# Storing q, k, y and the gate z as the vector engine leaves them, placing blocks at the load, and softmax sums sent to the gate through DRAM

## The chip, the cores and the metric

The kernel runs on one core of a Trainium2 chip. The metric is the time of one execution in device microseconds, the median of several runs. The engines are named as the profile names them: PE (matmul, with PEld for its weight loads), DVE (vector), ACT (scalar), POOL (GpSimd) and SP, which here does nothing but issue DMAs. All scratch tensors between the phases lie in the chip's DRAM (HBM).

## The reference

Two layers (DEPTH = 2) run over 2048 latent tokens and 256 context tokens of width 1024. A layer normalises and modulates the tokens, multiplies them by one input matrix (3344 columns), splits the columns among three groups of heads, and multiplies the concatenated outputs by one output matrix (condensed):

```python
(au, av, az, bq, bk, bv, bz, cq, ck, cv, co, cz, cg) = _split_proj(xn @ w_in)
y_b = softmax(q_lat @ k_all.T * scale) @ v_all * silu(bz)      # 8 heads of 64, 2 kv heads
y_c = sigmoid(co) * rms_norm(h_forward + h_backward) * silu(cz)  # mLSTM, 4 heads of 64
y_a = gelu(au) * (w_s @ layer_norm(gelu(av)) + b_s) * silu(az)   # gated MLP, 4 groups of 64
x = x + gt * (concatenate([y_a, y_b, y_c]) @ w_out)
```

Latent tokens attend to context and latent tokens (2304 keys), context tokens to the context alone, and the last layer has no context output.

## The kernel before

Tokens are cut into 18 tiles of 128 (2 of context, 16 latent), and tiles into blocks: the two context tiles, then four blocks of four latent tiles. A layer has three phases, and the next one's first work overlaps the last one's end.

**proj_phase** multiplies. It goes three times over six tiles each (a macro), and in each over seven groups of columns; a group's result for a tile is finished by a function of its own (post_c1 for the mLSTM's q and k, post_a2 for u and the attention's k, post_b1 for q, post_b2 for the gate z, ...), which ends with a store to DRAM through `ld`, so on SP's queue. Later phases want q, k and y transposed, with the features on partitions. DVE's transpose works on 32 by 32 blocks and leaves the blocks where they were, so `put_blocks` stores a tile with four DMAs, one for each group of 32 partitions, and each DMA puts its blocks of 128-byte pieces where they belong. During the third macro the mLSTM runs as well: `ml_state` walks over the tiles in both directions, and `ml_out` makes a tile's output. An ml_out loads sc, sct, sst, soz and two broadcast rows of snm (tile xt), POOL masks those rows, ACT exponentiates them, PE and DVE do the rest, and put_y stores the tile's y with eight of the DMAs of put_blocks (two chunks of 128 columns). At most three ml_out are alive at a time.

**attn_phase** works in units of one head and one block (32 a layer, and 8 for the context in the first layer). `unit_s` makes the scores of a unit (PE, 40 matmuls), DVE scales them and finds the maximum, ACT exponentiates and gives each row's sum (`den`). `unit_tr` transposes 128 keys of the unit on PE (18 steps of four transposes), and the copy is split in a rounded part and a rest: on odd steps by POOL (pT, lines 1119 and 1120), on even ones by DVE. `unit_mm` multiplies with v, five steps behind (LAG = 5). `unit_end` gates: for a pair of heads z is loaded as rows of tokens (tile sz), POOL multiplies each of the up to four tiles by 0.5/den (line 1148, the sum is a scalar of each partition there), PE transposes the gated z (line 1157), and DVE multiplies the output O with it.

**out_phase** loads a tile's y (tile yr, one DMA), splits it in two parts, multiplies with w_out, adds the residual.

PE multiplies fp32r with each operand split in two parts. The order of all instructions on an engine is fixed when the kernel is built, by a scheduler that simulates a timeline, so an engine that waits holds up everything behind it in its own order. SP too works its DMAs off in order, and a DMA whose data or buffer is not ready holds up those behind it.

## Time and profile before

| what | value |
|---|---|
| median of 3 runs | 3683.24 us (3678.11 to 3684.99) |
| the profiled execution: time, span | 3684.58 us, 3682.9 us |
| PE, DVE, ACT, POOL busy | 3582.6, 2556.9, 1942.0, 1892.3 us |
| granted clock of PE, mean | 0.988 |
| DMA packets | 531690, of them 297274 under 512 B |

The span runs from the first to the last instruction, and 1.7 us of the execution's time lie outside it. The first attention phase fills about 900 to 1700 us, the second about 2690 to 3470 us. The stretches in which the third macro and the mLSTM share the engines are about 640 to 920 us and 2480 to 2710 us. In the kernel before, line numbers of the profile are those of the listing above.

### The profile page before, as it was taken

How to read it: one execution, taken by the hardware profiler on the slowest of the kernel's cores; microseconds unless marked ns; L12 is line 12 of the kernel's file. 1: busy time of each engine (PE TensorE's matmuls, PEld its weight loads, DVE VectorE, ACT ScalarE, POOL GpSimd, SP SyncE). 2: the span in 40 equal slices, each digit the busy share in tenths (PEclk: the TensorE clock that was granted, in tenths of full speed). 3: DMA queues.
4: the chain of work that ended last, by engine and by line, in shares of the span. 5: the costliest groups of instructions: out<-in, count | busy, mean ns of one | idle time of the engine just before them, and what ended most of it. 6: DMA issues, size and time to landing. Idle time of an engine off the chain costs nothing.

```text
span 3682.9 us, 58371 instructions
## 1 busy us (share of the span) xinstructions
PE 3582.6 (97%) x19405; PEld 2937.3 (80%) x19405; DVE 2556.9 (69%) x6341; ACT 1942.0 (53%) x3409; POOL 1892.3 (51%) x2448
## 2 busy tenths in 40 slices
PE   8999999998999999999999999999999999999999
PEld 4877778776888888887788788877778888888787
DVE  4676664778888888887324636466888888888754
ACT  4223243334878788786114432432377877777621
POOL 2241342454777777776322524244557777777610
PEclk9999999999999999999999999999999999999999
DMA  7456455576001011002545553557720101100143
GB/s 216 137 138 175 138 129 136 159 194 156 25 28 37 17 35 43 24 12 95 175 121 151 132 148 83 141 145 180 174 57 18 31 27 35 35 24 10 58 148 113
DMA packets 531690, 359.21 MB, mean 98 GB/s; under 512 B 297274, under 2 KB 432178, under 8 KB 531388
## 3 DMA queue, kind: packets, MB, share of 16 engines
q1 hardware_dynamic: 518172, 336.05, 33.8%
q10 hardware_dynamic: 10368, 9.52, 0.8%
q0 software_dynamic: 2848, 9.91, 0.7%
q8 instruction: 154, 2.52, 0.3%
q14 instruction: 148, 1.21, 0.1%
HBM read 269.56 MB, written 85.76 MB: 96 GB/s over the span
## 4 chain that ended last, share of the span: by engine, by line
PE 69%; DMA 6%; DVE 4%; POOL 3%; issue 2%; SPq 2%; ACT 2%; DVEq 0%; POOLq 0%; ACTq 0%
PE acc L209 20%; PE m L1131 14%; PE acc L1096 14%; PE tr L1113 9%; PE x L209 6%; PE x L1113 4%; SPq L53 2%; DMA raw<-in_w_in_dram 1%; DMA xt<-snm 1%; DMA mkv<-sc 1%; DMA tab<-in_rope_dram 1%; DVE w L200 1%; DVE e L1098 1%; PE tr L476 0%; POOL pT L1120 0%
## 5 line engine op out<-in xcount | busy, mean ns | idle before, releaser
L209 PE MATMUL acc<-w,xn 128*128 128x512 f32 (+2 forms) x4728 | 1096.5, 385 | 5.3 <-POOL w L203 1.7
L209 PEld LDWEIGHTS acc<-w,xn 128*128 128x128 f32 x4728 | 844.2, 191 | 182.8 <-issue 5.4
L1098 DVE TENSOR_SCALAR_CACHE_REDUCE e<-acc,rqall 128x512 f32<-128x512 f32 (+1 forms) x1296 | 858.1, 690 | 144.4 <-PE acc L1096 76.6
L1131 PE MATMUL m<-pT,vst 128*128 128x512 f32 (+1 forms) x2336 | 775.3, 415 | 4.8 <-POOL pT L1120 4.0
L1096 PE MATMUL acc<-kst,qs 128*128 128x512 f32 (+1 forms) x2592 | 744.5, 385 | 11.6 <-DVE e L1098 10.0
L1120 POOL TENSOR_TENSOR pT<-pf,pT 128x512 fp32r<-128x512 f32 (+1 forms) x564 | 730.5, 1302 | 29.7
L1104 ACT ACTIVATE e<-e,nmx 128x2304 f32<-128x2304 f32 (+1 forms) x272 | 578.5, 2127 | 61.4 <-DVE nmx L1103 60.7
L1119 POOL TENSOR_SCALAR pT<-pf 128x512 fp32r<-128x512 f32 (+1 forms) x564 | 356.8, 636 | 338.5 <-ACT pf L1118 332.9
L1096 PEld LDWEIGHTS acc<-kst,qs 128*128 128x128 f32 x2592 | 447.4, 189 | 92.1 <-DVE e L1098 21.7
L1131 PEld LDWEIGHTS m<-pT,vst 128*128 128x128 f32 x2336 | 411.7, 189 | 65.6 <-POOL pT L1120 8.6
L1113 PE MATMUL tr<-ident,e 128*128 128x128 f32 x3084 | 456.9, 273 | 3.0 <-DVE pT L1123 2.1
L1113 PEld LDWEIGHTS tr<-ident,e 128*128 128x128 f32 x3084 | 375.1, 141 | 79.1 <-DVE pT L1123 4.0
L200 DVE TENSOR_TENSOR w<-raw,w 128x512 fp32r<-128x512 f32 (+1 forms) x276 | 205.5, 755 | 184.0 <-ACT w L199 182.3
L199 ACT CAST w<-raw 128x512 fp32r<-128x512 f32 (+1 forms) x276 | 161.6, 595 | 299.0 <-DMA raw<-in_w_in_dram 265.1
L1123 DVE TENSOR_TENSOR pT<-tr,pT 128x512 fp32r<-128x512 f32 x405 | 274.2, 683 | 59.5 <-ACT pT L1122 58.4
L209 PE MATMUL acc<-w,xs 128*128 128x512 f32 x1224 | 294.2, 398 | 1.7 <-DVE xs L249 1.3
L1122 ACT CAST pT<-tr 128x512 fp32r<-128x512 f32 x405 | 234.4, 587 | 95.2 <-PE tr L1113 79.8
L209 PEld LDWEIGHTS acc<-w,xs 128*128 128x128 f32 x1224 | 230.9, 189 | 58.3 <-DVE xs L249 1.7
L209 PE MATMUL x<-w,xn 128*128 128x512 f32 (+1 forms) x1128 | 263.3, 379 | 10.4 <-DVE w L200 6.0
L1118 ACT COPY pf<-tr 128x512 f32<-128x512 f32 (+1 forms) x372 | 214.5, 584 | 87.1 <-PE tr L1113 77.8
L202 POOL TENSOR_SCALAR w<-raw 128x512 fp32r<-128x512 f32 (+1 forms) x92 | 65.5, 712 | 361.7 <-PE acc L209 158.7
L209 PEld LDWEIGHTS x<-w,xn 128*128 128x128 f32 x1128 | 200.1, 190 | 54.8 <-DVE w L200 8.9
(282 smaller groups left out, 4402.9 us busy)
## 6 DMA issues: line engine op xcount, KB each, us to landing
raw<-in_w_in_dram SPq DMA_DIRECT2D x240, 256.0 KB, 3.1
raw<-in_w_in_dram SPq DMA_DIRECT2D x144, 128.0 KB, 2.4
mkv<-sc SPq DMA_DIRECT2D x68, 258.0 KB, 4.0
xt<-snm SPq DMA_DIRECT2D x68, 256.0 KB, 4.5
yr<-sy SPq DMA_DIRECT2D x34, 512.0 KB, 6.5
mst<-in_w_ada_dram SPq DMA_DIRECT2D x64, 256.0 KB, 3.7
qd<-sq SPq DMA_DIRECT2D x128, 128.0 KB, 2.8
xres<-xnew POOLq DMA_DIRECT2D x18, 512.0 KB, 5.2
```

The costliest lines, as they stand in the source:

```text
L200: V.tensor_tensor(wt[:, 1, :n], raw[:, :n], wt[:, 0, :n].bitcast(F32), op=ALU.subtract)
L209: T.matmul(acc[:, :n], xs[:, a, k, :], ws[k][:, b, c0:c0 + n], start=(k == 0 and j == 0), stop=(k == KC - 1 and j == 2))
L1096: T.matmul(acc[:, 0:w], u['qs'][:, r, j * P:(j + 1) * P], kf[:, c0:c0 + w], start=(r == 0), stop=(r == 1))
L1098: V.tensor_scalar(e[:, c0:c0 + w], acc[:, 0:w], rqall[:, u['tiles'][j], u['h']:u['h'] + 1], None, op0=ALU.mult, op1=ALU.max, accum_out=mx[ ...
L1104: A.activation(e[:, 0:nk], e[:, 0:nk], AF.Exp, bias=nmx, scale=1.0, accum_out=u['den'][:, j:j + 1])
L1113: T.transpose(tr[:, j * P:(j + 1) * P], u['e'][j][:, s * P:(s + 1) * P], ident)
L1118: A.copy(pf[:, 0:w], tr[:, 0:w])
L1119: G.tensor_scalar(pt_[:, 0, 0:w], pf[:, 0:w], 1.0, 0.0, op0=ALU.mult, op1=ALU.add)
L1120: G.tensor_tensor(pt_[:, 1, 0:w], pf[:, 0:w], pt_[:, 0, 0:w].bitcast(F32), op=ALU.subtract)
L1122: A.copy(pt_[:, 0, 0:w], tr[:, 0:w])
L1123: V.tensor_tensor(pt_[:, 1, 0:w], tr[:, 0:w], pt_[:, 0, 0:w].bitcast(F32), op=ALU.subtract)
L1131: T.matmul(u['o'][:, 0:w], vst[u['g']][:, s, :], pt_[:, r, 0:w], start=(s == 0 and r == 0), stop=(s == u['nk'] - 1 and r == 1))
```

## The change

Tiles that DVE has transposed by blocks are stored with one DMA, as they lie, and whoever loads them puts the blocks in place. For q and k, `load_twice` takes four DMAs of 128-byte pieces in place of two DMAs of whole rows. y of the groups A and C goes into one tensor for each tile (s_y) and is loaded with four DMAs (get_blocks) and one for the attention's y; the output matrix's rows are taken in the order YC to fit. The stores of the mLSTM's q and k keep four DMAs, with another layout in DRAM, and their load reads whole rows. The gate z is transposed by blocks on DVE after post_b2 and stored like q. In unit_end it is loaded already with features on partitions, by four DMAs, so the sums must lie along the free dimension: POOL doubles den, DVE takes the reciprocal, one DMA writes it to DRAM in pieces of 4 bytes (s_den), another reads it back as a row on 64 partitions (tile rd, two buffers), and POOL multiplies z by it. The transposes on PE are gone.

```diff
-    def put_blocks(rows, t):
-        for a in range(4):
-            o = slice(a * 32, a * 32 + 32)
-            ld(rows.rearrange("(b r) t -> r b t", r=32)[:, :, o], t[o].rearrange("r (b c) -> r b c", c=32))
+    def get_blocks(dst, src):
+        v = src.rearrange("(a r) (b n) -> r b a n", a=4, b=4)
+        for b in range(4):
+            ld(dst[b * 32:b * 32 + 32].rearrange("r (a n) -> r a n", a=4), v[:, b])
...
             def load_y(i):
-                yrs[i] = pt([P, KC, P], "yr", 2)
-                ld(yrs[i], part(g_y, i).rearrange("(k p) t -> p k t", p=P))
+                yrs[i] = pt([P, KC * P], "yr", 2)
+                get_blocks(yrs[i][:, 0:512], s_y[i])
+                ld(yrs[i][:, 512:1024].rearrange("p (k t) -> p k t", k=4), part4(g_y, i))
...
             def split_y(i):
-                A.copy(xs[:, 0], yrs[i])
-                V.tensor_tensor(xs[:, 1], yrs[i], xs[:, 0].bitcast(F32), op=ALU.subtract)
+                for sl, src in ((slice(0, 4), yrs[i][:, 0:512].rearrange("p (a k c) -> p k a c", a=4, k=4)),
+                                (slice(4, 8), yrs[i][:, 512:1024].rearrange("p (k a c) -> p k a c", a=4, k=4))):
+                    hi, lo = (xs[:, q, sl].rearrange("p k (a c) -> p k a c", a=4) for q in range(2))
+                    A.copy(hi, src)
+                    V.tensor_tensor(lo, src, hi.bitcast(F32), op=ALU.subtract)
...
             def put_y(i, t, chunk, kt=None):
-                V.transpose(yt[:, 0:256], t)
-                put_blocks(part(g_y, i)[chunk * P:(chunk + 2) * P], yt[:, 0:256])
+                yv = yt[:, 0:256].rearrange("p (b x c) -> p x b c", b=4, x=2)
+                V.transpose(yv, t[:, 0:256].rearrange("p (x b c) -> p x b c", b=4, x=2))
+                o = 0 if chunk == 0 else 64
+                ld(s_y[i].rearrange("p (b n) -> p b n", b=4)[:, :, o:o + 64],
+                   yt[:, 0:256].rearrange("p (b n) -> p b n", b=4))
                 if kt is not None:
                     V.transpose(yt[:, 256:384], kt)
-                    put_blocks(part(g_k, i), yt[:, 256:384])
+                    ld(row(g_k, i), yt[:, 256:384])
...
             def post_b1(i, acc, full):
                 V.transpose(sq, q.rearrange("p h d -> p (h d)"))
-                put_blocks(part(g_q, i), sq)
+                ld(row(g_q, i), sq)
...
             def post_b2(i, acc, full):
                 V.scalar_tensor_tensor(z, th, 1.0, acc, op0=ALU.add, op1=ALU.mult)
-                ld(part(g_z, i), z)
+                V.transpose(th, z)
+                ld(row(g_z, i), th)
...
             def load_twice(dst, src, n):
-                for q in range(2):
-                    ld(dst[q * HD:(q + 1) * HD, 0:n], src.rearrange("p a b -> p (a b)"))
+                v = src.rearrange("j (a r) (b c) -> r b (j a) c", a=4, c=32)
+                for q in range(4):
+                    ld(dst[q * 32:q * 32 + 32, 0:n].rearrange("r (a c) -> r a c", c=32), v[:, q % 2])
...
             def unit_end(u):
                 if q == 0:
-                    sz = pt([P, 4, P], "sz", 3)
-                    ld(sz[:, 0:n], g_z[b][:, :, u['h'] * HD:(u['h'] + 2) * HD])
-                    pairs[b] = sz, pt([P, 512], "O", 3)
-                V.reciprocal(u['den'][:, 0:n], u['den'][:, 0:n])
-                for j in range(n):
-                    G.tensor_scalar(sz[:, j, q * HD:(q + 1) * HD], sz[:, j, q * HD:(q + 1) * HD],
-                                    u['den'][:, j:j + 1], 0.5, op0=ALU.mult, op1=ALU.mult)
+                    z = pt([P, 512], "z", 3)
+                    zv = g_z[b].rearrange("j (a r) (b c) -> r b (j a) c", a=4, c=32)
+                    for k in range(4):
+                        ld(z[k * 32:k * 32 + 32, 0:w].rearrange("r (a c) -> r a c", c=32), zv[:, 2 * u['h'] + k])
+                    pairs[b] = z, pt([P, 512], "O", 3), pt([P, 512], "rd", 2)
+                G.tensor_scalar(u['den'][:, 0:n], u['den'][:, 0:n], 2.0, None, op0=ALU.mult)
+                V.reciprocal(u['den'][:, 0:n], u['den'][:, 0:n])
+                ld(s_den[b][u['h']].rearrange("o (j p) -> (o p) j", p=P), u['den'][:, 0:n])
+                ld(rd[r, 0:w], s_den[b][u['h']].to_broadcast([64, w]))
                 A.copy(O[r, 0:w], u['o'][rx, 0:w])
                 V.tensor_tensor(O[r, 0:w], u['o'][r, 0:w], O[r, 0:w], op=ALU.add)
+                G.tensor_tensor(z[r, 0:w], z[r, 0:w], rd[r, 0:w], op=ALU.mult)
                 if q == 1:
-                    tr = ptr()
-                    for j in range(n):
-                        T.transpose(tr[:, j * P:(j + 1) * P], sz[:, j, :], ident)
-                    V.tensor_tensor(O[:, 0:w], tr[:, 0:w], O[:, 0:w], op=ALU.mult)
+                    V.tensor_tensor(O[:, 0:w], z[:, 0:w], O[:, 0:w], op=ALU.mult)
```

SP's order, at the place where the third macro of the second layer and the mLSTM run together. The kernel before has this (sy and sq are stores of y and q from the tiles k, x4 stands for four DMAs; tab, raw, msc and mst are loads):

```order
L53 DMA m_5763_28359<-soz_173 128x256
L53 DMA sy_119<-k_5764_28387 32x8x32 x4
L53 DMA tab_28421<-in_rope_dram 128x128
L53 DMA sy_120<-k_5774_28441 32x8x32 x4
L53 DMA raw_28494<-in_w_in_dram 128x512
L53 DMA raw_28499<-in_w_in_dram 128x512
L53 DMA sq_111<-k_5744_28274 32x16x32 x4
L53 DMA msc_28501<-sct_143 128x4x128
```

After the change the same tiles (k_5764, k_5744) are stored so:

```order
L53 DMA xt_28121<-snm_271 128x512
L53 DMA sya_164<-k_5764_28316 512x1x64
L53 DMA sq_106<-k_5744_28206 128x512
L53 DMA mst_28184<-sst_4_238 128x2x65
L53 DMA mst_28184<-sst_4_256 128x2x65
L53 DMA m_5733_28124<-soz_230 128x256
L53 DMA raw_28414<-in_w_in_dram 128x512
```

Each x4 has become one DMA, and the loads behind it have moved up.

POOL's order in the first attention phase, where a unit ends. Before (pT are the split copies of the transposed scores, sz the gate):

```order
L1120 TENSOR_TENSOR pT_11932<-pf_11933,pT_11932 128x512
L1148 TENSOR_SCALAR sz_12515<-sz_12515,den_11645 128x64 x4
L1119 TENSOR_SCALAR pT_11971<-pf_11972 128x512
L1119 TENSOR_SCALAR pT_12001<-pf_12002 128x512
L1120 TENSOR_TENSOR pT_11971<-pf_11972,pT_11971 128x512
```

After, for the next unit of the same pair of heads:

```order
L1181 TENSOR_SCALAR den_11870<-den_11870 128x4
L1150 TENSOR_SCALAR pT_12156<-pf_12157 128x512
L1151 TENSOR_TENSOR pT_12156<-pf_12157,pT_12156 128x512
L1150 TENSOR_SCALAR pT_12197<-pf_12198 128x512
L1151 TENSOR_TENSOR pT_12197<-pf_12198,pT_12197 128x512
L1187 TENSOR_TENSOR z_12421<-z_12421,rd_12427 64x512
L1150 TENSOR_SCALAR pT_12227<-pf_12228 128x512
```

The four products have become one short instruction ahead of two pT pairs and one product behind them, which waits for rd; in 52 of the 72 units two pairs lie between, in 14 one or none, in 6 three or more. SP's order there has the way through DRAM among the loads of q and k for later units (qd) and of the next gate (z):

```order
L53 DMA rd_12427<-sden_0_136 64x512
L53 DMA qd_13350<-sk_152 32x8x32 x3
L53 DMA sy_177<-O_11787 128x512
L53 DMA qd_13350<-sk_152 32x8x32
L53 DMA sden_1_137<-den_11870 128x4x1
L53 DMA z_13754<-sz_111 32x16x32 x2
L53 DMA rd_12427<-sden_1_137 64x512
L53 DMA z_13754<-sz_111 32x16x32 x2
```

sden writes the sums to DRAM and rd reads them back, with two DMAs of the next z between; before, none of the two was there.

## Rows read from the trace of the kernel before

**Rows 1.** the page: busy us by engine over the span; the granted clock in 40 slices

```profile
PE 3582.6 (97%) x19405; PEld 2937.3 (80%) x19405; DVE 2556.9 (69%) x6341; ACT 1942.0 (53%) x3409; POOL 1892.3 (51%) x2448
...
PEclk9999999999999999999999999999999999999999
```

**Rows 2.** busy time by stretch: length, PE, PEld, DVE, ACT, POOL, clock, DMA

```profile
640.00:920.00 280.00, 256.48 (x1508) 199.43 (x1507) 214.68 (x598) 104.19 (x276) 136.45 (x199) 0.96 0.67 173
920.00:1680.00 760.00, 757.55 (x4551) 640.38 (x4550) 647.42 (x1776) 604.68 (x896) 559.62 (x683) 1.00 0.09 27
...
2480.00:2710.00 230.00, 213.90 (x1203) 167.15 (x1200) 183.60 (x502) 85.53 (x209) 109.04 (x155) 0.94 0.65 163
2710.00:3450.00 740.00, 739.36 (x4449) 628.93 (x4447) 615.32 (x1686) 585.33 (x837) 543.27 (x654) 1.00 0.08 24
```

**Rows 3.** chain of waits in 640 to 920 us, shares by line

```profile
by line: PE acc L209 15.3%; SPq L53 11.4%; DMA xt<-snm 9.5%; issue 8.0%; DMA mkv<-sc 6.7%; DMA sy<-k 3.0%; DMA tab<-in_rope_dram 2.3%; DVE xt L813 1.8%; DMA sst<-st 1.7%; DVE e L1098 1.7%; DMA gqb<-in_g_q_dram 1.6%; DMA vr<-sv 1.5%; ACT xt 
```

**Rows 4.** waits in 640 to 920 us: total us, times, longest

```profile
POOL xt L797 <- DMA xt<-snm: 33.4, 15, 5.5
...
POOL m L764 <- DMA mkv<-sc: 21.3, 10, 4.9
...
DVE k L615 <- POOL kss L131: 18.1, 6, 4.9
```

**Rows 5.** timeline of SP, 2600 to 2640 us: start, us, DMAs issued

```profile
2613.22 1.91 SPq L53 DMA_DIRECT2D sy<-k  x4
2615.40 0.35 SPq L53 DMA_DIRECT2D tab<-in_rope_dram  x1
2616.03 1.99 SPq L53 DMA_DIRECT2D sy<-k  x4
```

**Rows 6.** DMA issues in 640 to 920 us: count, KB, median us to landing

```profile
xt<-snm SPq DMA_DIRECT2D x32, 256.0 KB, 4.6
...
sy<-k SPq DMA_DIRECT2D x96, 32.0 KB, 2.1
...
sq<-k SPq DMA_DIRECT2D x24, 64.0 KB, 3.4
...
sk<-k SPq DMA_DIRECT2D x24, 16.0 KB, 2.8
```

**Rows 7.** timeline of PE in the first attention phase: start, us, instructions

```profile
970.61 0.60 PE L1157 MATMUL tr<-ident,sz 128*128 128x128 f32 x4
970.97 0.37 PE L1131 MATMUL m<-pT,vst 128*128 128x256 f32 x1
```

**Rows 8.** instructions on the tile sz: ns min/median/max

```profile
L1157 PE MATMUL tr<-ident,sz x96: 270/272/273, 970.6 to 3502.4; 128*128 128x128 f32 x96
...
L1157 PE MATMUL x<-ident,sz x40: 270/272/273, 1080.9 to 3355.6; 128*128 128x128 f32 x40
```

**Rows 9.** the page of DMA issues over the whole span

```profile
qd<-sq SPq DMA_DIRECT2D x128, 128.0 KB, 2.8
...
sq<-k SPq DMA_DIRECT2D x136, 64.0 KB, 2.2
...
sst<-st SPq DMA_DIRECT2D x68, 65.0 KB, 4.1
```

**Rows 10.** groups by line in 920 to 1680 us: busy us, mean ns, idle before

```profile
L1120 POOL TENSOR_TENSOR pT<-pf,pT 128x512 fp32r<-128x512 f32 x266 | 346.0, 1307 | 14.0
...
L1119 POOL TENSOR_SCALAR pT<-pf 128x512 fp32r<-128x512 f32 x267 | 169.9, 640 | 164.6 <-ACT pf L1118 159.8 <-DMA qd<-sq 2.6 <-PE m L1131 1.1
...
L1148 POOL TENSOR_SCALAR sz<-sz,den 128x64 f32<-128x64 f32 x134 | 41.8, 333 | 21.6 <-DVE den L1146 15.8 <-PE acc L1096 4.2 <-DVE nmx L1103 1.1
```

**Rows 11.** groups by line, whole span

```profile
L642 DVE STREAM_TRANSPOSE k<-k 128x512 f32<-128x512 f32 x34 | 24.0, 704 | 12.9 <-POOL k L600 12.7
...
L1146 DVE RECIPROCAL den<-den 128x4 f32<-128x4 f32 x64 | 11.1, 173 | 7.5 <-ACT e L1104 6.6 <-POOL pT L1120 0.6
```

**Rows 12.** instructions on the tile kst: ns min/median/max

```profile
L1067 POOL TENSOR_TENSOR kst<-qd,kst x6: 1275/1294/1567, 855.5 to 2667.9; 64x512 fp32r<-64x512 f32 x6
```

More of the change, by code (lines that the diff above doesn't have):

```diff
@@ L58, in ld, with late @@
         return r
+    def late(n=60):
+        return tc.high_priority(offset=-n)
     def nm(s):
@@ L137, in hybrid_kernel, with row, part4 @@
     where = {t: (bi, j) for bi, b in enumerate(blocks) for j, t in enumerate(b)}
-    g_z = [dram([P, len(b), 512], f"sz{i}") for i, b in enumerate(blocks)]
     g_v = [dram([P, len(b), 128], f"sv{i}") for i, b in enumerate(blocks)]
-    g_q = [dram([512, len(b), P], f"sq{i}") for i, b in enumerate(blocks)]
-    g_k = [dram([P, len(b), P], f"sk{i}") for i, b in enumerate(blocks)]
-    g_y = [dram([D, len(b), P], f"sy{i}") for i, b in enumerate(blocks)]
+    g_q = [dram([len(b), P, 512], f"sq{i}") for i, b in enumerate(blocks)]
+    g_z = [dram([len(b), P, 512], f"sz{i}") for i, b in enumerate(blocks)]
+    s_den = [[dram([1, len(b) * P], f"sden{i}_{h}") for h in range(8)] for i, b in enumerate(blocks)]
+    g_k = [dram([len(b), P, P], f"sk{i}") for i, b in enumerate(blocks)]
+    s_y = [dram([P, 512], f"sya{i}") for i in range(NT)]
+    g_y = [dram([P, 4, len(b), P], f"sy{i}") for i, b in enumerate(blocks)]
+    YC = (0, 1, 6, 7, 2, 3, 4, 5)
+    def row(grp, t):
+        bi, j = where[t]
+        return grp[bi][j]
+    def part4(grp, t):
+        bi, j = where[t]
+        return grp[bi][:, :, j, :]
     def part(grp, t):
@@ L497, in post_c1 @@
                     t = k2()
-                    V.transpose(t[:, 0:256], acc[:, 0:256])
-                    V.transpose(t[:, 256:512], kt)
+                    tv = t.rearrange("p (b x c) -> p x b c", b=4, x=4)
+                    V.transpose(tv[:, 0:2], acc[:, 0:256].rearrange("p (x b c) -> p x b c", b=4, x=2))
+                    V.transpose(tv[:, 2:4], kt.rearrange("p (x b c) -> p x b c", b=4, x=2))
                     yield
-                    put_blocks(s_t[i], t)
+                    for a in range(4):
+                        ld(s_t[i].rearrange("r b (x a c) -> r (b x) a c", x=4, a=4)[:, :, a],
+                           t[a * 32:a * 32 + 32].rearrange("r (m c) -> r m c", c=32))
             def post_c2(i, acc, full):
@@ L629, in post_a2 @@
                     V.transpose(kt, kv[:, 0:128])
-                    put_blocks(part(g_k, i), kt)
+                    ld(row(g_k, i), kt)
             def post_b1(i, acc, full):
@@ L810, in ml_out @@
                     for p in range(2):
-                        T.matmul(sT[:, p * P:(p + 1) * P], sc[r, 256 + p * P:256 + (p + 1) * P],
-                                 sc[r, p * P:(p + 1) * P], start=(p == 0), stop=(p == 1))
+                        T.matmul(sT[:, p * P:(p + 1) * P], qk[r, 2 + p], qk[r, p], start=(p == 0), stop=(p == 1))
                     V.tensor_tensor(at[:, :, q::2, :], dm[:, :, q::2, :],
@@ L820, in ml_out @@
                     for p in range(2):
-                        T.matmul(ip[:, p * 130:(p + 1) * 130], sc[r, p * P:(p + 1) * P],
+                        T.matmul(ip[:, p * 130:(p + 1) * 130], qk[r, p],
                                  stt[r, p].rearrange("p d e -> p (d e)"), start=(p == 0), stop=(p == 1))
@@ L1077, in unit_start @@
                 qd = pt([P, 512], "qd", 3)
-                load_twice(qd, g_q[where[tiles[0]][0]][h * HD:(h + 1) * HD], n * P)
+                load_twice(qd, g_q[where[tiles[0]][0]][:, :, h * HD:(h + 1) * HD], n * P)
                 qs = pt([P, 2, 512], "qs", 2, F32R)
```

13 lines of the change are left out of this document (7 added, 6 removed).

## The prediction, made before the changed kernel was run

> **What bounds the kernel now.** I read the page first: PE is busy 97% of the span and its clock is granted nearly throughout [rows 1], so time can be won only where PE does less or where it waits. Then the busy times by stretch [rows 2]. In the two attention phases PE is idle for 2.5 us of 760 and 0.6 us of 740, at full clock: there only less work for PE helps, and any new wait of PE costs its full length. In the two stretches in which the third macro runs beside the mLSTM, PE is idle for 280 - 256.5 = 23.5 us and 230 - 213.9 = 16.1 us. The granted clock averages 0.96 and 0.94 there, so part of the time PE runs at 1.2 instead of 2.4 GHz after its waits; that is worth another 0.04 x 280 = 11 us and 0.06 x 230 = 14 us. About 65 us are lost in these two stretches, and they are the only place of that size that this change touches.
>
> Why PE waits there I read from the chain of waits: SP's queue (11.4%) and the loads of snm and sc (9.5% and 6.7%) stand in it right behind PE's own matmuls [rows 3]. The waits show how it travels: POOL waits 33.4 us for snm and 21.3 us for sc, DVE waits 18.1 us for POOL [rows 4], and PE for DVE. SP's timeline shows DMAs issued one behind the other, and a store by put_blocks holds the queue for 1.91 to 1.99 us with its four DMAs, 0.5 us each [rows 5]. In 280 us there are 96 such DMAs for y, 24 for q and 24 for k [rows 6].
>
> **The change part by part.**
>
> *PE's transposes of the gate go.* There are 96 + 40 = 136 [rows 8]. Each lasts 272 ns, but they overlap: four start at 970.61 and the next matmul starts at 970.97 [rows 7], so one costs 0.36 / 4 = 0.09 us, and all cost 136 x 0.09 = 12.2 us. PE has no idle time in the attention phases that could swallow this. I take -12.
>
> The Trainium skill (TensorE: Matmul & The Clock Gate, Part 4: PE-mode transpose) gives about 275 ns for one transpose inside a kernel; the trace agrees with it as a duration (272 ns), not as a pace. By the page's figure the term would be an estimated 136 x 0.275 = 37 us.
>
> *SP issues fewer DMAs in the two stretches.* Stores of y, q and k go from four DMAs to one. Counted in SP's order from the store of snm to the last store of z, the first layer's stretch goes from 403 DMAs to 317 and the second's from 381 to 298, although the first loads of q, k and z for the attention, which lie there too, take more DMAs than before. At 0.5 us each that is 43 and 41 us of queue. The sum lies between nothing (the loads come earlier, but PE's order and DVE decide) and the whole 65 us. DVE is busy for 214.7 of 280 and 183.6 of 230 us [rows 2], which leaves room, but POOL and DVE also wait for each other. A fifth of SP's DMAs go, from a queue that has little pause; queueing shrinks by more than a fifth, and SP is one link of several. I take a third of the 65 us: -21.
>
> *DVE gets a transpose of z for every tile*, 0.70 us [rows 11], 34 in all. Twelve lie in the two stretches (6 tiles each): 8.4 us on an engine that is busy for 77 to 80% of them; half counted: +4, bounds 0 and 8. The other 22 lie in the first two macros, where PE's matmuls cover them. The transposes of y and of the mLSTM's q and k write to other addresses with the same count, taken as equal.
>
> *The attention's loads of q, k and z* take four DMAs each where there were two, two and one, and move 128-byte pieces. q is asked for as soon as one of three buffers comes free, two units of some 25 us ahead (740 us hold 4449 matmuls [rows 2], a unit has about 150). The load took 2.8 us [rows 9]; three more issues of 0.5 us leave it far from needed. DMA is busy for 8 to 9% there [rows 2]. 0; if the cover is gone, it would cost some 2 us for each first unit of a phase.
>
> *The way of the sums through DRAM.* Before, POOL multiplied four times 0.333 us, and waited 21.6 us before 134 of these, mostly for the reciprocal [rows 10]; over both phases some 40 us. Now POOL doubles den (at most 0.33 us by the same row) and multiplies z once (64 x 512, nearest row 1.29 us [rows 12]): 0.29 us more for each of 72 units, 21 us. The product must wait for the reciprocal (0.17 us [rows 11]), the store of 512 pieces and the load of 64 rows. No row shows 4-byte pieces. The nearest by count of pieces is the store of q, 512 pieces in 2.2 us, the far one that of sst, 4.1 us; the load is like qd, 2.8 us [rows 9], at the far end like xt<-snm, 4.6 us [rows 6]. With the near rows 0.17 + 2.2 + 2.8 = 5.2 us, with the far ones 8.9.
>
> POOL's order covers it with two pT pairs in 52 of 72 units: 2 x (0.64 + 1.31) = 3.9 us back to back, or 5.7 us at the present pace of 267 pairs in 760 us [rows 10]. So POOL waits 0 to 1.3 us there, and some 2.8 us in the 14 units with one pair or none: 52 x 0.65 + 14 x 2.8 = 73 us, less the 40 us that go, plus 21 us of work: about 54 us more on POOL. POOL is idle for 200 us of the first phase and 197 us of the second [rows 2]. Behind the product stand pT pairs that PE needs five steps later, so a wait is felt only where it outlasts that lead. I take a fifth: +10. Bounds: 0 and, with the far rows, 52 x 4.1 + 14 x 6.4 = 303 us.
>
> *The rest at nothing.* DVE's last product reads SBUF instead of PSUM, off PE's path. In out_phase the split of y comes in halves and y takes five DMAs; SP and ACT have long pauses there, and the next tile is loaded two tiles ahead. Uncovered it would be 4 x 0.5 = 2 us at each of the two phase starts. The last unit's sums are ready long before its matmuls end, so the start of out_phase does not wait for DRAM.
>
> Sum against the profiled execution: 3684.6 - 12 - 21 + 4 + 10 = 3665.6 us; against the median of 3683.2 (1.4 us lower) 3664 us.
>
> **The rivals.**
>
> *No relief where SP was crowded.* The third macro's end is decided by DVE and by the three ml_out that may be alive, each with loads of 4.6 us [rows 6]; the queue's gain is eaten by other waits. For it: DVE is near 80% there, and the order of PE is planned anew. Against it: SP's 11.4% of the chain. Then 3684.6 - 12 + 4 + 10 = 3687, no change that shows.
>
> *Slower: POOL stands at the product of z.* One mechanism, in attn_phase: the round trip outlasts two pT pairs, POOL holds its queue, pT comes late, and PE, with no slack, waits. It decides from 29 / 72 = 0.4 us of PE's waiting for each unit (29 us being -12 - 21 + 4). With a store of 4.1 us the way takes 7.1 us, POOL waits 52 x 2.3 + 14 x 4.6 = 184 us, 165 us more than now after the same correction; if a third reaches PE, 3684.6 - 29 + 55 = 3711. For it: the sums leave in 4-byte pieces, which no row has priced. Against it: pieces of 128 bytes land as fast as whole rows [rows 9], and POOL has a quarter of its time free.
>
> The Trainium skill (DMA: Bandwidth & Descriptors, Specifications and Rules for kernel authors) speaks for this rival: transfers below 512 B are read, modified and written, and a last dimension that isn't contiguous becomes one descriptor for each element. The store of q is below 512 B a piece as well and shows no such penalty in its 2.2 us.
>
> *More: a transpose costs PE its whole 272 ns* (it drains PE, and the matmuls beside it hide this in the timeline). Then the first term is 136 x 0.272 = 37 us, and the time 3684.6 - 37 - 21 + 4 + 10 = 3641.
>
> **How the numbers follow.** Forecast 0.56, no relief 0.20, slower 0.16, more 0.08. About 0.2% (7 us) is what a measurement of this kernel can tell from no change. The forecast's own range, 3645 to 3676, holds SP's share from a sixth to a half and POOL's from 0 to a third. The whole range, 3632 to 3706, takes in "more", "no relief" and the near half of "slower". Faster: 0.56 x 0.92 + 0.20 x 0.15 + 0.08 = 0.62; slower: 0.20 x 0.2 + 0.16 x 0.85 = 0.18; same 0.20.
>
> **What would show it.** Right: no matmul on z in the attention, PE still without idle time there, units about 0.2 us shorter on average; SP with pauses in the two stretches, POOL's waits for snm and sc well below 33 and 21 us, PE's idle time there below 40 us together. The store of sden lands in 2 to 3 us. Wrong: POOL's idle time before the product of z in the first places of its list with DMA rd as releaser, and PE waiting for pT by tens of us; or PE's idle time in the two stretches as before, with DVE as the releaser.

## The result, and the profile after

| | median | lowest to highest | ratio to before, 95% interval |
|---|---|---|---|
| before (4 runs) | 3680.68 us | 3677.24 to 3684.99 | |
| changed (4 runs) | 4415.48 us | 4411.72 to 4419.95 | 1.1996 (1.1975 to 1.2017) |

The changed kernel is 735 us slower; the prediction said 3664 us (3632 to 3706). Below, runs that were sent together shared a chip, on which the kernel before took 3669.7 to 3684.3 us, so versions are compared by their ratio to it; 0.1% is 3.7 us.

The page of the changed kernel, against [rows 1, 3]: busy times, the slices of PE and of its granted clock, and the chain that ended last.

```profile
span 4413.5 us, 58621 instructions
PE 3733.3 (85%) x19269; PEld 3033.1 (69%) x19269; DVE 2609.4 (59%) x6409; ACT 1949.7 (44%) x3443; POOL 1913.8 (43%) x2320
...
PE   8999999977777767777999999999677777777799
...
PEclk9999999988888888888999999999888888888899
...
PE 22%; DMA 11%; DVE 5%; issue 3%; POOL 3%; ACT 1%; SPq 1%; POOLq 0%; DVEq 0%; ACTq 0%
PE acc L228 9%; DMA sden<-den 6%; PE m L1162 4%; PE acc L1127 3%; PE x L228 3%; DMA rd<-sden 3%; PE tr L1144 2%; DVE e L1129 2%; POOL z L1187 1%; PE x L1144 1%; DMA xt<-snm 1%; POOL pT L1151 1%; DVE pT L1154 1%; SPq L53 1%; DVE qs L1112 0%
```

Before, PE was busy for 97% of the span [rows 1]; now it has two long dips, and its granted clock dips with it. They are the two attention phases. The store of the sums and the load of the row stand in the chain, which they could not do before. Windows of both phases and of the two stretches beside the mLSTM, changed kernel, then before (start and end, then busy us of PE, PEld, DVE, ACT, POOL, granted clock, DMA share, GB/s):

```profile
895.00:2120.00 1225.00, 913.09 (x4902) 754.65 (x4901) 722.95 (x1936) 663.24 (x988) 609.76 (x663) 0.86 0.14 27
3059.00:4237.00 1178.00, 893.33 (x4798) 738.37 (x4797) 699.08 (x1849) 643.72 (x925) 596.45 (x634) 0.87 0.14 26
637.00:895.00 258.00, 243.75 (x1458) 191.36 (x1457) 193.07 (x523) 87.73 (x249) 129.91 (x187) 0.97 0.68 182
2816.00:3059.00 243.00, 233.96 (x1390) 183.60 (x1389) 181.41 (x490) 82.01 (x230) 124.23 (x178) 0.97 0.70 183
```

```profile
891.00:1736.00 845.00, 832.57 (x4951) 697.48 (x4949) 713.63 (x1930) 660.19 (x988) 598.67 (x730) 1.00 0.12 35
2678.00:3505.00 827.00, 815.88 (x4843) 688.07 (x4842) 680.58 (x1839) 639.98 (x921) 578.97 (x695) 1.00 0.11 32
633.00:891.00 258.00, 241.30 (x1459) 190.62 (x1457) 193.22 (x519) 88.12 (x250) 132.15 (x187) 0.97 0.69 181
2427.00:2678.00 251.00, 240.12 (x1395) 188.73 (x1394) 185.08 (x491) 83.53 (x233) 126.58 (x180) 0.95 0.69 176
```

The phases grew by 380 and 351 us, which is the whole loss. PE's idle time there went from 12.4 + 11.1 to 311.9 + 284.7 us, 573 us more; the other 158 us are in its busy time (1806.4 for 1648.4 us), for fewer instructions, at a mean granted clock of 0.86 and 0.87: around the wait shown below, which ends at 1230.2 us, the granted clock is 0.5 (1.2 of 2.4 GHz) from 1223.7 to 1234.0 us. The stretches beside the mLSTM took 258 and 243 us, as against 258 and 251: the relief of SP shows nowhere in the first, and by 8 us at most in the second. POOL's wait for snm, which the prediction wanted well below 33 us, grew in the first (before, then changed: us in total, times, longest):

```profile
POOL xt L797 <- DMA xt<-snm: 34.8, 16, 5.5
```

```profile
POOL xt L828 <- DMA xt<-snm: 54.2, 15, 9.4
```

Waits of the first attention phase by engine (us in total, times, longest):

```profile
POOL z L1187 <- DMA rd<-sden: 336.6, 32, 18.5
...
PE m L1162 <- POOL pT L1150: 189.9, 25, 12.7
PE m L1162 <- POOL pT L1151: 101.8, 15, 16.8
...
SPq L53 <- DMA sden<-den: 355.8, 39, 10.8
```

And the timeline of one unit's end (start us, duration us; in brackets the idle time before, and what ended it):

```profile
1213.75 0.18 DVE L1182 RECIPROCAL den<-den 128x4 f32<-128x4 f32 x1 [0.16 <-POOL den L1181]
...
1213.99 0.38 SPq L53 DMA_DIRECT2D sden<-den  x1
...
1214.81 1.29 POOL L1151 TENSOR_TENSOR pT<-pf,pT 128x512 fp32r<-128x512 f32 x1
...
1219.66 0.71 PE L1127 MATMUL acc<-kst,qs 128*128 128x512 f32 x2
...
1223.47 0.45 SPq L53 DMA_DIRECT2D rd<-sden  x1
...
1228.32 1.25 POOL L1187 TENSOR_TENSOR z<-z,rd 64x512 f32<-64x512 f32 x1 [12.23 <-DMA rd<-sden]
...
1230.22 0.80 PE L1162 MATMUL m<-pT,vst 128*128 128x512 f32 x1 [9.84 <-POOL pT L1150]
```

The chain in four steps. The store goes out at 1213.99; SP issues the load that needs it at 1223.47, 9.5 us later; the row is there at 1228.32, after another 4.9 us; POOL, with one pT pair done meanwhile, has stood for 12.2 us, and PE for 9.8 us. Over the 72 units, read the same way, the store takes 9.8 us and the load 4.3 us in the median, together 14.2 us where the prediction had 5.2 (near rows) and 8.9 (far rows). And POOL stands for something that is not needed yet: in each of the 36 pairs DVE's product with O, the first to read the multiplied z, starts 29 us or more after the second head's product has ended (median 50 us).

### The profile page after: what moved, and what is told of

It reads as the page before. It is cut to its first block, busy times and chain, and to the rows that moved or that the text cites. A ratio compares the mean times of both kernels' runs of the same rounds, so it can differ in the third digit from the quotient of the medians.

```text
span 4413.5 us, 58621 instructions
## 1 busy us (share of the span) xinstructions
PE 3733.3 (85%) x19269; PEld 3033.1 (69%) x19269; DVE 2609.4 (59%) x6409; ACT 1949.7 (44%) x3443; POOL 1913.8 (43%) x2320
## 5 line engine op out<-in xcount | busy, mean ns | idle before, releaser
L1162 PE MATMUL m<-pT,vst 128*128 128x512 f32 (+1 forms) x2336 | 852.4, 449 | 565.9 <-POOL pT L1150 383.5
L1162 PEld LDWEIGHTS m<-pT,vst 128*128 128x128 f32 x2336 | 451.8, 208 | 661.4 <-POOL pT L1150 401.0
L1127 PE MATMUL acc<-kst,qs 128*128 128x512 f32 (+1 forms) x2592 | 794.0, 405 | 10.3 <-DVE e L1129 9.9
L1127 PEld LDWEIGHTS acc<-kst,qs 128*128 128x128 f32 x2592 | 481.1, 203 | 99.0 <-DVE e L1129 25.1
L1144 PE MATMUL tr<-ident,e 128*128 128x128 f32 x3094 | 488.8, 286 | 2.3 <-DVE pT L1154 0.9
L1144 PEld LDWEIGHTS tr<-ident,e 128*128 128x128 f32 x3094 | 404.6, 149 | 87.1 <-issue 12.1
L1187 POOL TENSOR_TENSOR z<-z,rd 64x512 f32<-64x512 f32 x72 | 86.2, 1197 | 729.0 <-DMA rd<-sden 626.5
L228 PE MATMUL acc<-w,xs 128*128 128x512 f32 x1224 | 298.0, 401 | 17.4 <-POOL w L221 14.2
L228 PE MATMUL x<-w,xn 128*128 128x512 f32 (+1 forms) x1128 | 261.2, 378 | 13.3 <-ACT w L218 6.6
L1144 PE MATMUL x<-ident,e 128*128 128x128 f32 x1546 | 245.4, 282 | 10.4 <-ACT pf L1149 5.9
```

What stands on the lines that cost most here:

```text
L228: T.matmul(acc[:, :n], xs[:, a, k, :], ws[k][:, b, c0:c0 + n], start=(k == 0 and j == 0), stop=(k == KC - 1 and j == 2))
L1127: T.matmul(acc[:, 0:w], u['qs'][:, r, j * P:(j + 1) * P], kf[:, c0:c0 + w], start=(r == 0), stop=(r == 1))
L1144: T.transpose(tr[:, j * P:(j + 1) * P], u['e'][j][:, s * P:(s + 1) * P], ident)
L1162: T.matmul(u['o'][:, 0:w], vst[u['g']][:, s, :], pt_[:, r, 0:w], start=(s == 0 and r == 0), stop=(s == u['nk'] - 1 and r == 1))
```

## The experiments

**Is it POOL's wait?** In e1_no_wait POOL's product takes a constant row; in e4_later everything waits as before, but the product is written 14 steps later and held behind the pT pairs ahead of it. The cuts of code below show the lines that matter; helpers and numbers of buffers are left out.

```diff
# e1_no_wait
-                G.tensor_tensor(z[r, 0:w], z[r, 0:w], rd[r, 0:w], op=ALU.mult)
+                G.tensor_tensor(z[r, 0:w], z[r, 0:w], half_row[r, 0:w], op=ALU.mult)
# e4_later: the same product, O's product and the store of y in rest(), run 14 calls of step_v later
+                todo.append([LATER, rest])
```

> The changed kernel, but POOL multiplies z by a constant row of 0.5 and not by the row that comes back from DRAM; the store of the sums and the load of the row are still issued. The division by the softmax sums is left out, only the wait is gone. Theory A (POOL stands at the product of z for a way of 14.2 us through DRAM, and everything lost in the attention phases follows from that): the phases, 1225 and 1177 us in the changed kernel, go back to at most the 845 and 827 us of the kernel before, less 12 us for the 136 transposes, so some 4415 - 380 - 350 - 12 = 3673 us (3660 to 3690). Theory B (the attention's own loads, four DMAs each with 128-byte pieces, or the 4-byte stores themselves, hold up PE or SP's queue): the time stays above 3900 us, because those transfers are all still there.

> The changed kernel with all its transfers and its waits, but the product of z (and behind it the last product and the store of y) is written 14 steps later and held behind the pT pairs before it in POOL's order; 14 steps of some 1.4 us are 19 us, more than the 14.2 us that the way through DRAM takes. Theory A: POOL no longer stands, the time is that of the version without the wait, about 3673 us. Theory B, or a wait that only moves to another place (SP's queue held by the load of the row, O or z buffers come free too late): above 3750 us.

Measured: e1_no_wait 3859.7 us, 1.0488 (1.0470 to 1.0506); e4_later 3751.8 us, 1.0185 (1.0168 to 1.0202). Without POOL's wait for the row three quarters of the loss are gone (0.151 of 0.200), so Theory A holds for most of it; but both versions stay well above 3673 us, so A alone is not enough (e1 lies below the 3900 us of Theory B, too). In e4's trace the product comes far later than the 19 us that were counted on: 62.7 us behind the issue of the store in the median, where the changed kernel had 14.2. SP's waits in e4_later's first phase, and those of ACT for the loads of k:

```profile
SPq L53 <- DMA sden<-den: 260.0, 32, 10.3
...
ACT kst L1097 <- DMA qd<-sk: 22.4, 5, 10.2
```

SP stands 8.1 us for each store, and the loads of q, k and z queue behind it. Whether that is the rest of the loss, the next two runs ask.

**Is the rest SP's standing, or the store itself?** e5_no_hold has e1's constant row, and its load reads a row that is long there, so that SP has nothing to wait for. e7_no_store has neither store nor load.

```diff
# e5_no_hold (on e1_no_wait)
-                ld(rd[r, 0:w], s_den[b][u['h']].to_broadcast([64, w]))
+                ld(rd[r, 0:w], s_c[2][0:1, 0:w].to_broadcast([64, w]))
# e7_no_store (on e5_no_hold): that line and the store into s_den taken out
```

> The version without the wait of POOL (constant row, division left out), in which the load of the row now reads another row of the same size that has long been written, so that SP's queue no longer holds for the store of the sums; the 4-byte store itself is still issued. Theory C (a second wait: SP issues in order, the load of the row stands there until the store has landed, 270 us in 33 waits of 8.2 us in the first attention phase of the version without POOL's wait, and the loads of z, q and k queue behind it): with SP free the attention phases fall to those of the kernel before less the transposes, and the time to about 3673 us (3660 to 3690). Theory B (the 4-byte stores or the 128-byte pieces load the DMA engines or DRAM so that everything else lands late): it stays near the 3860 us of the version without POOL's wait.

> The version without the wait for the row (constant row, division left out), now also without the store of the sums and without the load of the row: the gate's way through DRAM is gone altogether, the order of the code is that of the changed kernel and the product of z still stands right behind its load. Theory F (the 4-byte store holds the DMA queues for 8 to 10 us, whatever is issued behind it lands after it, and in the versions with a constant row POOL stands for the load of z instead: loads of z issued behind such a store landed 6.7 us later, others 2 us): with the store gone, POOL's wait for z falls from 72 and 83 us in the first phase to below 20 us and the time to 3690 to 3710 us. Theory G (the loads of z are late by themselves, four DMAs asked for only at the unit's end): it stays at 3850 us or more.

Measured: e5_no_hold 3883.7 us, 1.0556 (1.0535 to 1.0577); e7_no_store 3716.4 us, 1.0101 (1.0087 to 1.0115). Theory C fell: with SP free nothing was gained. Timeline of e5_no_hold around one pair's end:

```profile
1293.78 0.96 SPq L53 DMA_DIRECT2D z<-sz  x2
...
1294.97 0.38 SPq L53 DMA_DIRECT2D sden<-den  x1
1295.39 1.03 SPq L53 DMA_DIRECT2D z<-sz  x2
...
1302.65 1.25 POOL L1189 TENSOR_TENSOR z<-z,hr 64x512 f32<-64x512 f32 x1 [7.08 <-DMA z<-sz]
```

By the landings that the trace holds, the store landed at 1303.87, 8.9 us after its issue, and the two loads of z issued behind it, at 1295.39 and 1295.94, landed at 1304.46 and 1304.85, 9.1 and 8.9 us after theirs. POOL's product here waited for the two loads ahead of the store: one was there at 1296.72, but the last share of the other, issued at 1294.26, came at 1302.53, 8.3 us after its issue. Over the run, 30 loads of z that were issued while a store was under way landed after 9.1 us in the median; those with no store under way or just behind them (95 of the others) after 2.7 us. POOL's waits for z in the first phase, e5_no_hold, then e7_no_store:

```profile
POOL z L1189 <- DMA z<-sz: 83.1, 12, 28.6
```

```profile
POOL z L1187 <- DMA z<-sz: 21.6, 10, 7.5
```

Taking the store away took 62 of these 83 us and 167 us of the time. So Theory F stands in its main point, with both its numbers just missed (21.6 for 20 us, 3716 for at most 3710). e7 lacks the load of the row as well as the store; what that load costs by itself was not tried. The Trainium skill (DMA: Bandwidth & Descriptors, Queues, rings and completion order) says that a DMA's completion mark is written only after every earlier write of the same DMA engine. The 9.1 us of the loads behind the store agree with it; the late share of the load ahead of the store is not covered by it.

**What makes the store slow?** e3_pieces16 stores the four numbers of a partition side by side, and POOL reads the row with a stride; e6_forms stores in another form for each head.

```diff
# e3_pieces16
-                ld(s_den[b][u['h']].rearrange("o (j p) -> (o p) j", p=P), u['den'][:, 0:n])
+                ld(s_den[b][u['h']].rearrange("o (p j) -> (o p) j", j=n), u['den'][:, 0:n])
```

> The changed kernel, but the sums leave as 128 pieces of 16 bytes, the four numbers of a partition side by side, in place of 512 pieces of 4 bytes; POOL reads the row with a stride. Same bytes, same wait. If the store's 9.8 us go by the number of pieces (19 ns each): about 2.5 us, the way is some 7 us, POOL's wait falls by 7 of 10 us a unit, and the time by 72 x 7 us, to about 3900 us. If the store's time is a fixed cost of writing into a few neighbouring addresses, it stays near 9.8 us and the time near 4400 us.

> The price of the store by itself, in a kernel that does not use the row: each head stores in another form, and one 4-byte load behind it, which waits for the store, shows when it has landed. Forms: 512 pieces of 4 bytes side by side; the same 128 bytes apart; the same 512 bytes apart; 128 pieces of 16 bytes side by side; 256 pieces of 4 bytes side by side; 128 pieces of 4 bytes side by side; 128 pieces of 128 bytes; 512 pieces of 128 bytes. Theory D (the number of pieces sets the time, 19 ns each): 9.8, 9.8, 9.8, 2.1, 4.9, 2.5, 2.5 and 9.8 us. Theory E (small writes into the same neighbourhood wait for each other, as the store of q with 512 pieces of 128 bytes landed in 2.2 us): 9.8, about 2, about 2, 2.1, 5, 2.5, 2 and 2.2 us. The time of the whole kernel is no matter here.

e3_pieces16 took 3767.2 us, 1.0228 (1.0214 to 1.0242): below the 3900 us of its expectation; the store lands in 2.0 us and the row 3.3 us behind it (medians of 72). e6_forms (3748.1 us, a single run) gives the price. Each pair of rows of SP's timeline is a store and the small load that waits for it; the forms are, in order, 512 pieces of 4 bytes side by side, 512 of 4 bytes 128 bytes apart, 512 bytes apart, 128 pieces of 16 bytes side by side, and 128 of 4 bytes side by side:

```profile
1231.68 0.38 SPq L53 DMA_DIRECT2D sden<-den  x1
1241.12 0.23 SPq L53 DMA_DIRECT2D rd<-sden  x1
1256.53 0.38 SPq L53 DMA_DIRECT2D sden<-den  x1
1258.77 0.23 SPq L53 DMA_DIRECT2D rd<-sden  x1
1282.90 0.38 SPq L53 DMA_DIRECT2D sden<-den  x1
1284.68 0.23 SPq L53 DMA_DIRECT2D rd<-sden  x1
1309.05 0.38 SPq L53 DMA_DIRECT2D sden<-den  x1
1310.80 0.23 SPq L53 DMA_DIRECT2D rd<-sden  x1
...
1571.74 0.49 SPq L53 DMA_DIRECT2D sden<-den  x1
1579.24 0.23 SPq L53 DMA_DIRECT2D rd<-sden  x1
```

9.4, 2.2, 1.8, 1.8 and 7.5 us; 256 of 4 bytes side by side took 8.7 us. Over the eight stores of each form the medians are 9.5, 2.2, 1.8, 2.0 and 7.8 us, and 8.4 for the 256. The same 512 pieces cost 9.5 us packed and 2 us spread, and a quarter of them packed still costs 7.8. Theory D, the count of pieces, fell; Theory E names what the rows show, that the time goes by where the 4-byte pieces lie, but not in proportion to their number (it had 5 and 2.5 us for 256 and 128), and pieces of 16 bytes side by side are not slow. How the small writes hold each other up no run shows. The two forms with 128-byte pieces were issued at the start of the phases among other DMAs and give no price.

**Both cures.** f1_16_later is the changed kernel with 16-byte pieces and the product 14 steps later; f2_gate_only has the gate's new way with these cures on the old layouts of q, k, y and the mLSTM; g2_gate_6 and i3_all_6 are f2 and f1 with 6 steps, and none once a phase's last scores are made.

```diff
# g2_gate_6, i3_all_6
-                todo.append([LATER, rest])            # LATER = 14
+                todo.append([LATER if more else 0, rest])   # LATER = 6
```

> The changed kernel with both cures: 16-byte pieces, so that the store lands in 2 us and SP is held 2 and not 10 us, and the product of z 14 steps later. With Theories A and C together nothing is left that waits: about 3675 us, the kernel before with 12 us of transposes less and a few us more for DVE's transposes of z. If the small pieces of the attention's loads cost something by themselves: 3700 us or more.

> The kernel before with the gate's new way alone (z transposed by DVE and stored so, 16-byte pieces, product 14 steps later); q, k, y and the mLSTM's tiles keep the four stores each of the kernel before. As the new layout with the old gate was 12 us slower than the kernel before (3696 to 3684), this should be some 12 us faster than the version with both cures: 3663 us. If the 12 us were the luck of a different order in the first stretches, it equals that version within 5 us.

> The kernel before with the gate's new way alone (16-byte pieces, product later), the product now 6 steps later (8 us, the way takes 6 us) and not later at all once the last scores of a phase are done, where POOL has no pT pairs. If the 14 steps cost something at the ends of the phases, where the store of y follows the product: 5 us less than the 3685 us with 14 steps, 3680 us. If not, 3685 us; if 6 steps don't cover the way, POOL's wait for the row is back and the time above 3695 us.

> The changed kernel with all its layouts and the best cures: 16-byte pieces, product 6 steps later and none late at a phase's end. With 14 steps it stood at 1.0072; the gate alone went from 1.0008 to 0.9973 by the same step. If the layouts of q, k, y and the mLSTM cost the same beside either: 1.0037. If their cost is no property of theirs but of the order that the scheduler makes of each version: anywhere from 0.997 to 1.010.

| version | median | ratio, 95% interval |
|---|---|---|
| f1_16_later | 3709.5 us | 1.0072 (1.0059 to 1.0085) |
| i3_all_6 | 3692.6 us | 1.0036 (1.0024 to 1.0049) |
| f2_gate_only | 3685.0 us | 1.0008 (0.9999 to 1.0017) |
| **g2_gate_6** | **3670.2 us** | **0.9973 (0.9964 to 0.9982)** |

g2_gate_6 is faster than both kernels, by 10 us and 745 us; the 10 us were measured on one chip. Its attention phases:

```profile
881.00:1724.00 843.00, 829.67 (x4902) 695.85 (x4901) 720.86 (x1938) 657.63 (x986) 629.38 (x665) 1.00 0.17 41
2663.00:3485.00 822.00, 810.45 (x4790) 682.17 (x4789) 694.96 (x1841) 637.90 (x921) 608.13 (x632) 1.00 0.15 37
```

PE is idle for 13.3 and 11.6 us, as before the change, at full clock: the wait is gone, the transposes stay away. POOL stands 2.8 us in all before its 72 products. They come 50.8 us behind the issue of the store in the median, so "6 steps" are far more than the 8 us that were counted on, and how short the distance may be was not tried. Of the 19.8 us by which the profiled execution is shorter than that of before, 5.9 lie in the two attention phases (842.9 + 822.8 us from the first score matmul to the last V matmul, for 844.8 + 826.8); 8.8 lie ahead of the first store of snm (623.8 and 632.6 us), where none of the removed transposes was.

**What do the other layouts cost?** e2_old_gate is the changed kernel with the gate as before; g3_gate_qk is f2 with the new layout of q and k, g4_gate_y f2 with that of y and the mLSTM's tiles.

```diff
# e2_old_gate: g_z, post_b2 and unit_end as before, all else as changed
# g3_gate_qk (on f2_gate_only): g_q, g_k, load_twice as changed
-                put_blocks(part(g_q, i), sq)
+                ld(row(g_q, i), sq)
# g4_gate_y (on f1_16_later): the same lines put back, all else as changed
```

> The changed kernel with the gate's way undone: z is stored as rows again, POOL scales it by den, PE transposes it; q, k, y and the mLSTM's q and k keep the new layout with one store and placing loads. If the stores of y, q and k relieve SP to some effect, as the prediction had it with 21 us: about 3660 us. If SP's queue did not bound the stretches beside the mLSTM (between the first store of snm and the first attention matmul there lie 258.2 us before and 258.3 us in the changed kernel): 3675 to 3690 us, no difference from the kernel before. Theory B above would have it slower than the kernel before by tens of us or more.

> The kernel before with the gate's new way (16-byte pieces, 14 steps later) and the new layout of q and k alone: one store each instead of four, four placing loads with 128-byte pieces in the attention instead of two. All layouts together cost 24 us (3709 to 3685). If q and k carry it (the attention's loads with more DMAs): about 3705 us. If y and the mLSTM's tiles carry it: about 3685 us.

> The complement: the gate's new way (16-byte pieces, 14 steps later) and the new layouts of y and of the mLSTM's q and k, while q and k of the attention keep four stores and two loads. If y and the mLSTM's tiles carry the 24 us: about 3705 us. If q and k carry them: about 3685 us. If the 24 us are no part's own, but come of the new order of the stretches: both near 3695 us, or one of them off the sum by 10 us or more.

Measured: e2_old_gate 3696.1 us, 1.0035 (1.0021 to 1.0048); g3_gate_qk 3695.0 us, 1.0040 (1.0025 to 1.0056); g4_gate_y 3722.7 us, 1.0117 (1.0103 to 1.0130). The layouts cost 0.35% beside the old gate (e2), 0.64% beside the new one (f1 less f2) and again 0.63% (i3 less g2): they are a loss, of 13 to 23 us, not a gain of 21. Alone, q and k cost 0.32% and y with the mLSTM 1.09%; these don't add up to 0.64%, which points to the order that the scheduler makes of each version; that was not tried by itself. Nor did SP's relief show here: from the first store of snm to the first score matmul the two stretches took 266 and 254 us in e2 (258 and 251 before), and 259 and 248 us in i3 (257 and 245 in g2).

**Why does less work for SP give nothing?** i1_bytes adds to g2_gate_6, in each ml_out right ahead of the loads of snm, a copy of 256 KB within DRAM; i2_dmas adds four of 512 bytes there. (In h1_more_bytes and h2_more_dmas the same copies had no predecessor and were issued in the kernel's first 60 us; both gave 1.001 and tell nothing of the stretches; their first store of snm comes at 633.6 and 634.8 us, for 623.8 in g2.)

```diff
# i1_bytes
+                behind_la(ld(s_x[i], w_in[l, 0:64, 0:1024]))
# i2_dmas
+                for k in range(4):
+                    behind_la(ld(s_x[i][k:k + 1, 0:128], w_in[l, k:k + 1, 0:128]))
```

> The copy of 256 KB within DRAM again, 36 in all, in the version that beat both kernels, but now kept in SP's order behind the mLSTM's state loads of its ml_out and so right ahead of the loads of snm; in the two runs before, the extra DMAs had no predecessor and went out at the start of the kernel (27.9 to 61.3 us of the span), so that they tell nothing of the stretches. The version itself is at 0.9973 of the kernel before. Theory H (bytes in the DMA queues set when snm arrives): a third to all of 36 x 256 KB at 180 GB/s = 52 us shows, ratio 1.002 to 1.012. Theory I (SP's issues set it): 36 x 0.5 us at most, ratio 0.998 to 1.002.

> The four DMAs of 512 bytes for each ml_out again, now at the same place: 2 us of SP's queue for each ml_out and hardly a byte, 72 us of queue in all. Theory I: a third or more of it shows, as the prediction took a third of what it saw lost there: ratio 1.004 or more. Theory H: ratio 0.996 to 1.000.

Measured: i1_bytes 3700.4 us, 1.0059 (1.0045 to 1.0073), 32 us more than g2; i2_dmas 3738.6 us, 1.0160 (1.0146 to 1.0174), 69 us more. There are 34 places, not 36. In the profiled executions the two stretches are 21 us longer in i1 (269.2 + 254.4 for 257.3 + 245.3) and 71 us longer in i2 (293.3 + 280.6). Neither theory has it alone: bytes cost what H said, and SP's issues at this place cost most of the 83 us that they took of SP's queue, which H excluded. What the removed DMAs were worth is another matter, since they stood elsewhere. One ml_out in each kernel, from SP's timeline and POOL's (the select is the first work on the loaded snm), before, changed, i2_dmas:

```profile
811.48 0.38 SPq L53 DMA_DIRECT2D msc<-sct  x1
...
813.75 1.01 SPq L53 DMA_DIRECT2D xt<-snm  x2
...
818.41 0.64 POOL L797 TENSOR_SCALAR_AFFINE_SELECT xt<-xt 128x512 f32<-128x512 f32 x1 [2.58 <-DMA xt<-snm]
```

```profile
855.23 0.55 SPq L53 DMA_DIRECT2D msc<-sct  x1
...
856.40 1.00 SPq L53 DMA_DIRECT2D xt<-snm  x2
...
862.79 1.06 POOL L828 TENSOR_SCALAR_AFFINE_SELECT xt<-xt 128x512 f32<-128x512 f32 x1 [5.77 <-DMA xt<-snm]
```

```profile
758.68 0.43 SPq L53 DMA_DIRECT2D msc<-sct  x1
...
762.64 2.50 SPq L53 DMA_DIRECT2D sx<-in_w_in_dram  x4
...
765.18 1.05 SPq L53 DMA_DIRECT2D xt<-snm  x2
...
769.07 0.64 POOL L808 TENSOR_SCALAR_AFFINE_SELECT xt<-xt 128x512 f32<-128x512 f32 x1 [6.47 <-DMA xt<-snm]
```

Over the 18 ml_out of the first layer (medians): snm is issued 2.5 us behind sct before, 1.2 in the changed kernel, 5.6 in i2_dmas; the first of its two loads is there 4.4, 5.8 and 3.9 us after its issue, and 7.0, 7.8 and 9.6 us after the issue of sct. SP's lead of 1.3 us in the changed kernel is one of order (in most ml_out of before the two loads of sst stand between, in the changed kernel they don't), and it is gone when snm lands: the loads of one ml_out come closer together, the DMA queues are as busy as before (0.68 for 0.69), and the last load lands no sooner. That the DMA queues are what it runs into is read from these rows and fits i1_bytes; it was not tried with fewer bytes. DMAs put in between, however, delay snm by all of their 2.5 us.

**What does a transpose of PE cost?** h3_transposes puts the 136 transposes back into g2_gate_6, into PSUM that nobody reads.

```diff
+                        tr = ptr()
+                        for j in range(n):
+                            T.transpose(tr[:, j * P:(j + 1) * P], z[:, j * P:(j + 1) * P], ident)
```

> The same version with PE's transposes put back: at the end of each pair PE transposes the four tiles of z, 136 in all, into PSUM, and nobody reads them. If a transpose costs PE its pace of 0.09 us: 3670 + 12 = 3682 us. If it costs its 272 ns: 3707 us. If PE had room for it: 3670 us.

Measured: 3712.8 us, 1.0118 (1.0101 to 1.0135), 1.45% or 53 us more than g2 by the ratios, which were taken on two chips; in the profiled executions the two attention phases are 42 us longer (859.9 + 848.1 for 842.9 + 822.8). Either is more than both prices. Its timeline on PE still shows the fast pace:

```profile
966.06 0.60 PE L1169 MATMUL tr<-ident,z 128*128 128x128 f32 x4
966.49 0.60 PE L1116 MATMUL tr<-ident,e 128*128 128x128 f32 x4
```

0.43 us for four, 36 x 0.43 = 15 us in all. PE's busy time in the phases is 21 us more, and another 21 us are idle time (46 for 25 us by the windows). The transposes wait in PE's order for a product of another engine and take a PSUM buffer in turn with the transposes of e, so this run prices more than the transposes. That PE has no room for them is shown, their size is not settled by it.

## Why the prediction was wrong

**The step that failed is the way of the sums through DRAM: +10 us, bounds 0 to 303; the runs showed about +730.** The mechanism was named, as the rival "POOL stands at the product of z", with the right place, releaser and break-even; the forecast gave it 0.16 and a price of 3711 us. Three sizes in it were off. The way takes 14.2 us, not 5.2 to 8.9: the store takes 9.8, and the far row's 4.1 was no bound, since no row of before had pieces of 4 bytes side by side. POOL's standing is 729 / 72 = 10.1 us a unit (its idle time before the product), not 2.3. And nearly all of it reaches the time, not a fifth or a third: with the row's wait taken away (e1_no_wait) POOL's idle time before the product fell by 593 us (729 to 136) and the two phases by 565 us. The lead of five steps had been counted as a cover, but every pT pair behind the product waits in POOL's order, and PE has no slack [rows 2] to win a stand of 10 us back: it was idle for 573 us more, and its busy time grew by 158 us at the lower granted clock. The rest of the loss, which e1 keeps, is for the most part the late landing of other loads (below).

The Trainium skill's two warnings (DMA: Bandwidth & Descriptors, Specifications and Rules for kernel authors), small transfers and a last dimension that isn't contiguous, were set aside in the prediction by the row of q's store. Neither gives a price. The packed store's 9.8 us would fit them, but so would 512 pieces of 4 bytes that lie 128 bytes apart, and these took 2.2 us.

**SP issues fewer DMAs, -21 us: wrong, the layouts cost 13 to 23 us.** The rival "no relief" was right. The step that failed is the share of a chain of waits taken for a gain: SP's 11.4% [rows 3] were time in which SP was the last link, and in the changed kernel snm lands no sooner although it is issued sooner. That the DMA queues are the link that takes SP's place is argued, not shown. Why the layouts even lose stays open, but the traces show where: of the 25 us between the profiled executions of g2 and i3, 11 come before the first store of snm (623.8 and 635.0 us), in the first two macros, where the prediction had put nothing, 5 in the two stretches, and 9 in the second attention phase (822.8 and 831.7 us).

**PE's transposes, -12 us: the sign fits, the size isn't shown.** g2_gate_6 shows -10 us (-7 to -13) for the gate's new way with its waits cured, near -12 + 4, but this is partly luck: its two attention phases, the only place where the transposes stood, are 5.9 us shorter, with 7.6 us less busy time of PE, and the rest of its gain lies elsewhere. With the other layouts the phases even grew, from 1670.3 us with the old gate (e2) to 1675.4 us with the new one (i3). The rival "more" (-37) is not what g2 gained, and h3's 42 to 53 us, which price more than the transposes, don't decide for it.

**DVE's transposes of z, +4, and the attention's loads at nothing.** The first was not tried by itself. The second was wrong by little: q and k's new way alone costs 0.32%, 12 us, though part of that may be order.

**What the prediction did not have.** The store does not only come late itself, it makes other loads late: without POOL's wait the kernel was still 4.9% slower than before, and 1.0% once the store was gone too.

**A slip that decides nothing.** With SP's share from a sixth to a half and POOL's from 0 to a third, the prediction's own terms reach from 3643 to 3682 us, not from 3645 to 3676.

## What to carry to other kernels

Before a small result goes through DRAM, look at how its pieces lie there: four numbers side by side in place of one took the store from 9.8 to 2.0 us here, and the loads of z issued behind it from 9.1 to 3.5 us (e5_no_hold and e3_pieces16, medians of 30 and 6). An instruction that waits for DRAM belongs farther behind its request, in its engine's order, than the way takes, measured and not assumed: the scheduler put it two pT pairs behind here, and its result was not needed for another 29 us or more. And a queue's share in the chain of waits is not what its relief is worth: ask which link stands next at the same moment.

## What the runs showed of the hardware that was not expected

- 4-byte writes to DRAM side by side: 512 in 9.5 us, 256 in 8.4, 128 in 7.8; 512 of them 128 or 512 bytes apart in 2.2 and 1.8 us; 128 of 16 bytes side by side in 2.0 us (e6_forms, medians of eight).
- Loads of z issued while such a store was under way landed 9.1 us after their issue, others of the same kind after 2.7 us (e5_no_hold, medians of 30 and 95).
- Four DMAs of 512 bytes (2.5 us of SP) right ahead of a load on the path made the two stretches 71 us longer for 34 places, one copy of 256 KB at the same place 21 us (i2_dmas and i1_bytes against g2_gate_6).
